# A one-core decoder trunk: buffer rings of five panels, sums first in seven-product squares, low-rank stages moved

## The chip, the cores and the metric

The kernel runs on one core of a Trainium2 chip. The metric is the device time of one execution in microseconds; before the change it is 1195.39 us, the median of three runs (1192.28 to 1196.88). In the profile PE is TensorE's matmul, PEld its weight loads, DVE VectorE, ACT ScalarE, POOL GpSimd and SP the engine that issues most DMAs.

## The reference

One layer on 256 tokens of width 2048, in float32. The input projection feeds a pooling mixer and an RWKV-7 mixer of 16 heads of 64; a squared-ReLU FFN of width 8192 and a gated embedding follow.

```python
h = rms_norm(x, attn_norm)
z = h @ w_in
zs = token_shift(z[..., POOL_WIDTH:IN_WIDTH], mu_shift)      # r, k, v, then the low-rank w, a, g
d = causal_multiscale_pool(z[..., :POOL_WIDTH])
pool_out = einsum('btgc,gcd->btgd', d, pool_w) * pool_scale
# rwkv7_time_mix:
decay = exp(-exp(-softplus(-(w0 + tanh(zw) @ w_up)) - 0.5))
a = sigmoid(a0 + za @ a_up);  g = sigmoid(zg) @ g_up
kk = normalized(k * k_k);  k = k * (1 + (a - 1) * k_a)
y = wkv7_scan(r, decay, k, v, -kk, kk * a)                   # a recurrence over the tokens
y = group_norm(y) * gn_g + gn_b + sum(r * k * r_k) * v
x = x + concat([pool_out, y * g]) @ w_out
x = x + square(relu(rms_norm(x, mlp_norm) @ w_ffn_up)) @ w_ffn_down
x = x + sigmoid(rms_norm(x, ple_norm) @ w_ple_gate) * (p @ w_ple_proj)
return rms_norm(x, final_norm)
```

## The kernel before

Weights come from HBM as panels of 128 x 1024 floats (512 KB). `load_raw` issues the load on SP's queue into a "raw" buffer. `split_w` splits the panel in a high part (`wh`, a copy on ACT in two halves, L165) and a low part (`wl`, raw less high, on DVE, L166). The activations are split in the same way, and each product is three matmuls: high by high, low by high, high by low. The buffers come from rings: `ring` takes one of three `wp` buffers of its tag, and once the pool `fp` exists (in the FFN and after it) every fourth request takes a buffer from that pool, so a ring has four there.

**The front part** overlaps two kinds of work on PE. Products of z are generators in a list `queue`: zk0, zr0, zk1, zr1, zv0, zv1, then the pool products zp0, zp1 (k, r and v for the two groups of eight heads, 0 and 1). `fill(us)` lets the head of the list emit matmuls worth that many us by its own estimate, `finish(p)` empties the list up to the end of one product. Between them stand the calls of the RWKV stages, written by hand. `rwkv_lora(gi)` makes the decay's running products `P` and `EI` and the rate `aa` of one group: two pairs of matmul groups `lw` and `la` (L521), eight sigmoids on ACT (L524, L525), four scans on DVE (L528) and two Exp (L530, L531). `rwkv_k` squares k (L542), sums per head on PE (`kkn`), takes the norm, spreads it (`rnb`), and builds the factors `AR` and `BK` of the scores (L560 to L584). `rwkv_scores` (L613) and `rwkv_scores_half` (L642) multiply them, `rwkv_sources` makes transposed sources, `bonus_sums` (`bsum`) and `bonus` (`bon`, L755) the bonus term, `rwkv_values` (`vt`, L769) the centred values. `rwkv_core` runs the recurrence in chunks of 64 tokens; `group_norm` (L880 to L884) scales its output and `group_out` (`yt`, L890) transposes it. When a product of z ends, its two PSUM banks are emptied by L322 on ACT and L323 on DVE.

**The FFN** goes by halves of the hidden width. `gemm_wide` makes the up product. `sweep` makes the down product, two times for each half (d00, d01, d10, d11), over 16 pairs of panels each. Pairs 1, 3, ..., 13 are squares by seven products in place of eight: `weights_seven` forms four sums `t` of blocks of the two raw panels `ra` and `rb` (L1226, L1231, L1232), high parts (`ha`, `hb` in the wh ring, `th`) and low parts (`la`, `lb` in the wl ring, L1229 and L1235; `tl`, L1236). The other pairs are plain (`split_w`). The residual of a sweep is formed in a tile `u`.

**The tail** makes the gate's product with eight panels kept in SBUF (`keep`), in buffers that the FFN has left, and the final norm.

What orders the instructions of an engine: the framework's scheduler places them by the order of the program and by priority. `tc.high_priority(n)` moves instructions ahead on their engine. A buffer is reused when its last reader is done, and the wait for that stands in the engine's queue, in order.

Of the kernel before, what the change touches and what calls it, by code (L numbers as in the profile page):

```python
# [9 lines left out]
F32 = mybir.dt.float32  # L10
F32R = mybir.dt.float32r
AF = mybir.ActivationFunctionType
ALU = mybir.AluOpType
# [27 lines left out]
def trunk(  # L41
# [19 lines left out]
    nc = tc.nc  # L61
# [81 lines left out]

    extra = []
    turns = {"raw": 0, "wh": 0, "wl": 0, "mm": 0}

    def ring(tag, dt, name):

        if extra:
            turns[tag] += 1  # L150
            if turns[tag] % 4 == 0:
                return extra[0].tile([128, 1024], dt, tag=f"{tag}x", name=name)
        return wp.tile([128, 1024], dt, tag=tag, name=name)

    def load_raw(src, n, name):
        raw = ring("raw", F32, f"raw_{name}")
# [852 lines left out]

    fill(3.0)  # L1010
    wag_out()
    fill(14.0)
    st0 = rwkv_lora(0)
    finish(p_zk0)
    wband = make_bands()
    rwkv_k(0, st0, zk0[0])
    finish(p_zr0)
    rwkv_r(0, st0, zr0[0])
    fill(7.0)
    rwkv_scores(0, st0)  # L1020
    rwkv_sources(0, st0)
    bonus_sums(0, st0)
    st1 = rwkv_lora(1)
    finish(p_zk1)
    rwkv_k(1, st1, zk1[0])
    fill(12.0)
    rwkv_scores_half(1, st1, 0)
    sts = (st0, st1)
    beside += [inverse(sts), 1.0, 0.0]
# [3 lines left out]
    rwkv_scores_half(1, st1, 1)  # L1033
    rwkv_sources(1, st1)
    finish(p_zv0)
    fill(4.0)
    rwkv_values(0, st0, zv0[0])
    bonus_sums(1, st1)
    while beside:
        fill(1.0)  # L1040
    fill(2.4)
# [9 lines left out]
    ds0 = pool_chunk(0, zt0[0])  # L1051
    for gi in range(2):
        group_out(gi, 0, norms[0][gi], YTs[gi])
    fill(4.0)
    for gi in range(2):
        group_out(gi, 1, norms[1][gi], YTs[gi])
    mgs = []
# [92 lines left out]
        nc.vector.reciprocal(s2, s2)  # L1150

    kept = []
    keep_at = ["ys"] * 3 + ["a5", "th", "tl", "t", "U"]

    def keep():
        kp = len(kept)
        where = keep_at[kp]
        raw = load_raw(w_gate[3, kp].rearrange("p a n -> p (a n)"), 1024, f"gk{kp}")
        if where == "ys":
            wh, wl = (fp.tile([128, 1024], F32R, tag=where, bufs=7, name=f"gk{kp}{c}") for c in "hl")  # L1160
# [55 lines left out]
    def weights_seven(ra, rb, name):  # L1216

        b12, b21, b22 = rb[:, 0:512], rb[:, 512:1024], ra[:, 512:1024]
        t, th, tl = (
            fp.tile([128, 4, 512], dt, tag=tg, name=f"{tg}_{name}") for tg, dt in (("t", F32), ("th", F32R), ("tl", F32R))  # L1220
        )
        ha, hb = (ring("wh", F32R, f"w7h{i}_{name}") for i in range(2))
        la, lb = (ring("wl", F32R, f"w7l{i}_{name}") for i in range(2))
        with tc.high_priority(20000):
            nc.scalar.activation(ha, ra, AF.Copy)
            nc.vector.tensor_tensor(  # L1226
                t[:, 0:2], ra.rearrange("p (c n) -> p c n", c=2), b12.unsqueeze(1).to_broadcast([128, 2, 512]), op=ALU.subtract
            )
            nc.vector.tensor_tensor(la, ra, ha.bitcast(F32), op=ALU.subtract)  # L1229
            nc.scalar.activation(th[:, 0:2], t[:, 0:2], AF.Copy)  # L1230
            nc.vector.tensor_tensor(t[:, 2], b22, t[:, 0], op=ALU.add)  # L1231
            nc.vector.tensor_tensor(t[:, 3], b21, t[:, 2], op=ALU.subtract)  # L1232
            nc.scalar.activation(hb[:, 0:512], b21, AF.Copy)
            nc.scalar.activation(th[:, 2:4], t[:, 2:4], AF.Copy)  # L1234
            nc.vector.tensor_tensor(lb[:, 0:512], b21, hb[:, 0:512].bitcast(F32), op=ALU.subtract)  # L1235
            nc.vector.tensor_tensor(tl, t, th.bitcast(F32), op=ALU.subtract)  # L1236

        def half(h_, l_, c):
            return h_[:, c * 512 : (c + 1) * 512], l_[:, c * 512 : (c + 1) * 512]

        return {
            "b11": half(ha, la, 0), "b22": half(ha, la, 1), "b21": half(hb, lb, 0),
            **{nm: (th[:, c], tl[:, c]) for c, nm in enumerate(("t1", "t3", "t2", "t4"))},
        }

    def sweep(src, acts, np_, name, residual_, hooks=()):
# [22 lines left out]
        for i in range(npair):  # L1269
# [3 lines left out]
            if i in SEVEN:  # L1273
# [8 lines left out]
                    ):  # L1282
                        step(which, o, a(f), w[t], fin and which != "p4")
                if fin:
                    u = fp.tile([128, 4, 512], F32, tag="U", name=f"u_{name}")
                    with tc.high_priority(30000):
                        nc.scalar.activation(u[:, 0], p1, AF.Copy)
                        nc.vector.tensor_tensor(u[:, 1], p6, u[:, 0], op=ALU.add)
# [16 lines left out]

    def scaled_residual(n, tt, src, wide=512):
        xs = xr[tt][:, n * 512 : n * 512 + wide]
        with tc.high_priority(10000 if wide > 512 else 30000):
            nc.vector.scalar_tensor_tensor(xs, src, s2[:, tt : tt + 1], xs, op0=ALU.mult, op1=ALU.add)

    def ffn_half(hf):
# [187 lines left out]
```

## Time and profile before

| | us |
| --- | --- |
| runs | 1195.39, 1196.88, 1192.28 (median 1195.39) |
| the profiled execution | 1192.48 |
| its span | 1190.8 |
| PE, PEld busy | 1164.7, 996.4 |
| DVE, ACT busy | 855.4, 678.7 |
| granted TensorE clock, mean | 0.997 |

The span runs from the first to the last instruction; the rest of the 1192.48 lies around it. Busy time is the union of an engine's instructions; matmuls overlap in PE, and their ends are modelled, so their cadence is read from starts. A row of the waits names the engine and line that waited, what it waited for, the sum in us, how often, and the longest. A row of the timeline has the start, the duration in us, the engine, the line, the operation, its output and inputs, and in brackets the idle time in front of it with what ended it.

The windows of the trace give PE's busy time by stage, from the span's start:

```text
window            PE busy   DVE busy  ACT busy
0 to 130          120.17    92.64     90.83      start, zk0, zr0, zk1, part of zr1
130 to 325        190.65   134.41    116.25      rest of the mixers, first part of w_out
325 to 570        244.84   157.32    129.43      w_out, first FFN up
570 to 1090       516.55   410.96    285.23      FFN: down 0, up 1, down 1
1090 to 1191       92.53    60.07     56.94      gate, final norm
```

### The profile page before, as it was taken

The page shows a single profiled execution, that of the slowest core. Times are in us where ns is not written, and L with a number is a line of the kernel's source. Part 1 is how long each engine was busy: PE and PEld are TensorE (multiplying, and loading weights), DVE is VectorE, ACT ScalarE, POOL GpSimd, SP SyncE. Part 2 cuts the span into 40 slices and gives each one's busy share as a digit, 9 for nine tenths or more (in the row PEclk, how much of TensorE's full clock was granted, in tenths as well). Part 3 has the DMA queues.
Part 4 walks back from the last instruction along what each step waited for, and adds up shares of the span by engine and source line. Part 5 has one row for each costly group of instructions (what it writes and reads, how often), then busy time and mean ns, then how long its engine had stood idle before and what let it go on. Part 6 is the DMA issues. An engine that isn't in the chain of part 4 may idle for free.

```text
span 1190.8 us, 18955 instructions
## 1 busy us (share of the span) xinstructions
PE 1164.7 (98%) x7366; PEld 996.4 (84%) x7366; DVE 855.4 (72%) x1073; ACT 678.7 (57%) x1210; POOL 20.1 (2%) x77
## 2 busy tenths in 40 slices
PE   7999999999999999999999999999999999999997
PEld 5899999787888888888878888888888788887886
DVE  6885799356655666667788887666668789888753
ACT  5956765667555554555554554554546554568643
POOL 4100000000000000000000000000000000000000
PEclk9999999999999999999999999999999999999999
DMA  7353434454566556565455656555555565666831
GB/s 267 124 187 124 155 125 142 143 175 138 191 184 191 178 180 191 182 190 182 172 212 185 217 204 210 193 181 190 185 187 163 208 208 186 218 246 201 274 125 71
DMA packets 60618, 216.92 MB, mean 182 GB/s; under 512 B 6768, under 2 KB 7536, under 8 KB 60144
## 3 DMA queue, kind: packets, MB, share of 16 engines
q1 hardware_dynamic: 60240, 215.20, 54.8%
q8 instruction: 58, 0.95, 0.3%
q10 hardware_dynamic: 288, 0.51, 0.1%
q14 instruction: 32, 0.26, 0.1%
HBM read 213.59 MB, written 2.10 MB: 181 GB/s over the span
## 4 chain that ended last, share of the span: by engine, by line
PE 73%; DVE 5%; DMA 2%; ACT 1%; issue 1%; DVEq 0%; ACTq 0%
PE u_w L1104 20%; PE d_p L1173 13%; PE u_w L1108 10%; PE d_w L1173 5%; PE d_d L1173 3%; PE o_b L188 2%; PE o_b L187 2%; PE o_b L189 2%; PE gt_b L187 2%; PE gt_b L189 2%; PE gt_b L188 2%; DVE wl_d L166 2%; DMA raw_d<-in_w_ffn_down_dram 2%; PE zp_b L187 1%; PE zp_b L189 1%
## 5 line engine op out<-in xcount | busy, mean ns | idle before, releaser
L1104 PE MATMUL u_w<-h,wh_u 128*128 128x512 f32 x1024 | 362.1, 399 | 0.0
L1108 PE MATMUL u_w<-h,wl_u 128*128 128x256 f32 x1024 | 287.7, 281 | 0.0
L165 ACT ACTIVATE wh_u<-raw_u 128x512 fp32r<-128x512 f32 x256 | 147.4, 624 | 175.6 <-issue 136.7
L166 DVE TENSOR_TENSOR wl_u<-raw_u,wh_u 128x1024 fp32r<-128x1024 f32 x128 | 156.6, 1224 | 120.9 <-ACT wh_u L165 120.9
L1104 PEld LDWEIGHTS u_w<-h,wh_u 128*128 128x128 f32 x1024 | 192.5, 188 | 47.8
L1108 PEld LDWEIGHTS u_w<-h,wl_u 128*128 128x128 f32 x1024 | 193.4, 189 | 0.0
L1173 PE MATMUL d_p<-wh_d,yd 128*128 128x512 f32 x432 | 115.6, 389 | 0.0
L1173 PEld LDWEIGHTS d_p<-wh_d,yd 128*128 128x128 f32 x432 | 81.0, 188 | 16.6
L165 ACT ACTIVATE wh_d<-raw_d 128x512 fp32r<-128x512 f32 x144 | 79.7, 619 | 23.4 <-PE d_d L1173 12.0
L166 DVE TENSOR_TENSOR wl_d<-raw_d,wh_d 128x1024 fp32r<-128x1024 f32 x72 | 85.1, 1219 | 2.3 <-ACT wh_d L165 2.2
L1236 DVE TENSOR_TENSOR tl_d<-t_d,th_d 128x2048 fp32r<-128x2048 f32 x28 | 64.2, 2292 | 29.3 <-ACT th_d L1234 29.3
L1173 PE MATMUL d_p<-wl_d,yd 128*128 128x512 f32 x216 | 68.5, 393 | 2.8 <-DVE wl_d L166 2.8
L1234 ACT ACTIVATE th_d<-t_d 128x1024 fp32r<-128x1024 f32 x28 | 29.7, 1060 | 69.1 <-DVE t_d L1232 69.1
L166 DVE TENSOR_TENSOR wl_o<-raw_o,wh_o 128x1024 fp32r<-128x1024 f32 x32 | 39.1, 1225 | 35.9 <-ACT wh_o L165 35.9
L165 ACT ACTIVATE wh_o<-raw_o 128x512 fp32r<-128x512 f32 x64 | 36.7, 624 | 32.4 <-PE o_b L188 18.4
L1173 PEld LDWEIGHTS d_p<-wl_d,yd 128*128 128x128 f32 x216 | 40.5, 188 | 14.2 <-DVE wl_d L166 6.1
L1226 DVE TENSOR_TENSOR t_d<-raw_d,raw_d 128x1024 f32<-128x1024 f32 x28 | 34.2, 1222 | 14.4 <-DMA raw_d<-in_w_ffn_down_dram 14.4
L1173 PE MATMUL d_w<-th_d,ys 128*128 128x512 f32 x168 | 42.6, 389 | 0.0
L1230 ACT ACTIVATE th_d<-t_d 128x1024 fp32r<-128x1024 f32 x28 | 29.7, 1060 | 17.9 <-DVE t_d L1226 14.7
L178 PE MATMUL zv_b<-hTh,wh_zv 128*128 128x256 f32 x128 | 37.8, 295 | 1.3 <-DVE zv_t L323 1.3
L178 PE MATMUL zr_b<-hTh,wh_zr 128*128 128x256 f32 x128 | 36.7, 287 | 2.0 <-DVE zk_t L323 2.0
L1173 PE MATMUL d_d<-wh_d,yd 128*128 128x512 f32 x144 | 38.5, 389 | 0.0
(445 smaller groups left out, 2529.5 us busy)
## 6 DMA issues: line engine op xcount, KB each, us to landing
raw_u<-in_w_ffn_up_dram SPq DMA_DIRECT2D x128, 512.0 KB, 3.5
raw_d<-in_w_ffn_down_dram SPq DMA_DIRECT2D x128, 512.0 KB, 4.4
raw_o<-in_w_out_dram SPq DMA_DIRECT2D x32, 512.0 KB, 3.5
raw_gt<-in_w_ple_gate_dram SPq DMA_DIRECT2D x24, 512.0 KB, 4.4
raw_zk<-in_w_in_dram SPq DMA_DIRECT2D x16, 512.0 KB, 4.1
raw_zr<-in_w_in_dram SPq DMA_DIRECT2D x16, 512.0 KB, 3.5
raw_zv<-in_w_in_dram SPq DMA_DIRECT2D x16, 512.0 KB, 3.5
raw_zp<-in_w_in_dram SPq DMA_DIRECT2D x16, 512.0 KB, 3.5
```

The costliest lines, as they stand in the source:

```text
L165: nc.scalar.activation(wh[:, a * 512 : (a + 1) * 512], raw[:, a * 512 : (a + 1) * 512], AF.Copy)
L166: nc.vector.tensor_tensor(wl, raw, wh.bitcast(F32), op=ALU.subtract)
L178: nc.tensor.matmul(o, w_h, ah, start=first and ct % 2 == 0, stop=False, skip_group_check=True)
L187: nc.tensor.matmul(o, a_h, wh[:, 0:n], start=first, stop=False)
L188: nc.tensor.matmul(o, a_l, wh[:, 0:n], start=False, stop=False)
L189: nc.tensor.matmul(o, a_h, wl[:, 0:n], start=False, stop=last)
L1104: nc.tensor.matmul(bank[:, ct, :].rearrange("p (s t) -> p s t", s=2), wh[:, c], hl, start=k == 0, stop=False, skip_group_check=True,)
L1108: nc.tensor.matmul(bank[:, ct, 0:T], wl[:, c], hl[:, 0, :], start=False, stop=k == 15, skip_group_check=True)
L1173: nc.tensor.matmul(o, l, r, start=first, stop=last, skip_group_check=True)
L1226: nc.vector.tensor_tensor(t[:, 0:2], ra.rearrange("p (c n) -> p c n", c=2), b12.unsqueeze(1).to_broadcast([128, 2, 512]), op=ALU.subtract)
L1230: nc.scalar.activation(th[:, 0:2], t[:, 0:2], AF.Copy)
L1236: nc.vector.tensor_tensor(tl, t, th.bitcast(F32), op=ALU.subtract)
```

## The change

Six edits, in the order of the program. (a) The rings of raw and wh get two buffers from `fp` in place of one (five in all); wl keeps three and one. Within a ring the extra buffers are now named by their turn, and turns are counted from the start. (b) The stages of group 0 and 1: `rwkv_lora(0)` moves behind `finish(p_zk0)` and `make_bands`, with two new fills of 3; the fill of 14 ahead of it goes. `rwkv_lora(1)` moves ahead of `rwkv_sources(0)`, and the fill ahead of the first half of the scores of group 1 goes from 12 to 13. (c) `bonus_sums(1)` moves ahead of `rwkv_values(0)`. (d) The fill between the two pairs of `group_out` goes from 4 to 5.3. (e) In `weights_seven` the two sums come before the low parts in the program. (f) `u` takes the buffer of `t`; the tag "U" goes, one kept gate panel has its low part in "yd", and the wide residual's priority is 25000.

```diff
     extra = []
     turns = {"raw": 0, "wh": 0, "wl": 0, "mm": 0}
+    RING = {"raw": (3, 2), "wh": (3, 2), "wl": (3, 1)}
 
     def ring(tag, dt, name):
 
-        if extra:
-            turns[tag] += 1
-            if turns[tag] % 4 == 0:
-                return extra[0].tile([128, 1024], dt, tag=f"{tag}x", name=name)
-        return wp.tile([128, 1024], dt, tag=tag, name=name)
+        n, m = RING[tag]
+        turns[tag] += 1
+        if extra and turns[tag] % (n + m) >= n:
+            return extra[0].tile([128, 1024], dt, tag=f"{tag}x", bufs=m, name=name)
+        return wp.tile([128, 1024], dt, tag=tag, bufs=n, name=name)
...
     wag_out()
-    fill(14.0)
-    st0 = rwkv_lora(0)
     finish(p_zk0)
     wband = make_bands()
+    fill(3.0)
+    st0 = rwkv_lora(0)
+    fill(3.0)
     rwkv_k(0, st0, zk0[0])
     finish(p_zr0)
     rwkv_r(0, st0, zr0[0])
     fill(7.0)
     rwkv_scores(0, st0)
+    st1 = rwkv_lora(1)
     rwkv_sources(0, st0)
     bonus_sums(0, st0)
-    st1 = rwkv_lora(1)
     finish(p_zk1)
     rwkv_k(1, st1, zk1[0])
-    fill(12.0)
+    fill(13.0)
     rwkv_scores_half(1, st1, 0)
...
     finish(p_zv0)
+    bonus_sums(1, st1)
     fill(4.0)
     rwkv_values(0, st0, zv0[0])
-    bonus_sums(1, st1)
...
         group_out(gi, 0, norms[0][gi], YTs[gi])
-    fill(4.0)
+    fill(5.3)
     for gi in range(2):
         group_out(gi, 1, norms[1][gi], YTs[gi])
...
-    keep_at = ["ys"] * 3 + ["a5", "th", "tl", "t", "U"]
+    keep_at = ["ys"] * 3 + ["yd", "a5", "th", "tl", "t"]
...
-            nc.vector.tensor_tensor(la, ra, ha.bitcast(F32), op=ALU.subtract)
-            nc.scalar.activation(th[:, 0:2], t[:, 0:2], AF.Copy)
             nc.vector.tensor_tensor(t[:, 2], b22, t[:, 0], op=ALU.add)
             nc.vector.tensor_tensor(t[:, 3], b21, t[:, 2], op=ALU.subtract)
+            nc.scalar.activation(th[:, 0:2], t[:, 0:2], AF.Copy)
             nc.scalar.activation(hb[:, 0:512], b21, AF.Copy)
+            nc.vector.tensor_tensor(la, ra, ha.bitcast(F32), op=ALU.subtract)
+            nc.vector.tensor_tensor(lb[:, 0:512], b21, hb[:, 0:512].bitcast(F32), op=ALU.subtract)
             nc.scalar.activation(th[:, 2:4], t[:, 2:4], AF.Copy)
-            nc.vector.tensor_tensor(lb[:, 0:512], b21, hb[:, 0:512].bitcast(F32), op=ALU.subtract)
             nc.vector.tensor_tensor(tl, t, th.bitcast(F32), op=ALU.subtract)
...
-                    u = fp.tile([128, 4, 512], F32, tag="U", name=f"u_{name}")
+                    u = fp.tile([128, 4, 512], F32, tag="t", name=f"u_{name}")
...
-        with tc.high_priority(10000 if wide > 512 else 30000):
+        with tc.high_priority(25000 if wide > 512 else 30000):
```

How this moves instructions is shown at three places. A row has the line, the operation, the output and the inputs, the shape, and a count where equal rows follow each other; numbers behind a name tell buffers apart. Lines of the changed kernel are one to three higher than before. First ACT, in the seam from zk0 to zr0, before: `lw` and `la` are the low-rank products, L322 empties the banks of zk0.

```order
L165 ACTIVATE wh_zr_0_690<-raw_zr_0_688 128x512 x2
L524 ACTIVATE tA_t<-lw,par_sb 128x256 x2
L525 ACTIVATE tD_t<-la,par_sb 128x256 x2
L564 ACTIVATE tE_t<-tD_t,oka,par_sb 128x256 x2
L524 ACTIVATE tA_t<-lw,par_sb 128x256 x2
L525 ACTIVATE tD_t<-la,par_sb 128x256 x2
L530 ACT_TABLE_LOAD
L530 ACTIVATE tA_t<-tB_t 128x1024
L165 ACTIVATE wh_zr_1_721<-raw_zr_1_719 128x512 x2
L322 ACTIVATE zk_t<-zk_b_339,omu 128x256
L531 ACTIVATE tC_t<-tB_t 128x1024
L322 ACTIVATE zk_t<-zk_b_340,omu 128x256
```

The same stretch of ACT in the changed kernel (L323 here is L322 of before):

```order
L166 ACTIVATE wh_zr_0_648<-raw_zr_0_646 128x512 x2
L166 ACTIVATE wh_zr_1_679<-raw_zr_1_677 128x512 x2
L323 ACTIVATE zk_t<-zk_b_339,omu 128x256 x2
L323 ACTIVATE zk_t<-zk_b_340,omu 128x256
L166 ACTIVATE wh_zr_2_744<-raw_zr_2_742 128x512 x2
L323 ACTIVATE zk_t<-zk_b_340,omu 128x256
L166 ACTIVATE wh_zr_3_783<-raw_zr_3_781 128x512 x2
L525 ACTIVATE tA_t<-lw,par_sb 128x256 x2
L526 ACTIVATE tD_t<-la,par_sb 128x256 x2
```

The copies out of zk0's banks now stand ahead of the low-rank stage. Second PE, around the transposes `yt` of the second half of the tokens, before:

```order
L890 MATMUL yt<-ident,ys_2747 128x128 x4
L187 MATMUL zp_b_2928<-wh_zp_7_3330,hTh_153 128x512
L188 MATMUL zp_b_2928<-wh_zp_7_3330,hTl_155 128x512
L189 MATMUL zp_b_2928<-wl_zp_7_3331,hTh_153 128x512
L187 MATMUL zp_b_2928<-wh_zp_7_3330,hTh_153 128x512
L188 MATMUL zp_b_2928<-wh_zp_7_3330,hTl_155 128x512
L189 MATMUL zp_b_2928<-wl_zp_7_3331,hTh_153 128x512
L890 MATMUL yt<-ident,ys_2746 128x128 x4
```

and in the changed kernel (L891 is L890 of before):

```order
L952 MATMUL pd_3399<-wband,zt_2899 128x128
L891 MATMUL yt<-ident,ys_2752 128x128 x4
L891 MATMUL yt<-ident,ys_2753 128x128 x4
L891 MATMUL yt<-ident,ys_2752 128x128 x4
L891 MATMUL yt<-ident,ys_2753 128x128 x4
L910 MATMUL gt<-zf,gu_2721 128x256 x4
```

The six matmuls of zp1 no longer stand between the two pairs of transposes; they come earlier. Third DVE, in the first down sweep, one square (pair 5) and the plain pair 4 ahead of it, before:

```order
L1226 TENSOR_TENSOR t_d_5_6166<-raw_d_0_5_6162,raw_d_1_5_6164 128x1024
L166 TENSOR_TENSOR wl_d_0_4_6129<-raw_d_0_4_6124,wh_d_0_4_6128 128x1024
L166 TENSOR_TENSOR wl_d_1_4_6134<-raw_d_1_4_6126,wh_d_1_4_6133 128x1024
L1229 TENSOR_TENSOR w7l_d_5_6171<-raw_d_0_5_6162,w7h_d_5_6169 128x1024
L1231 TENSOR_TENSOR t_d_5_6166<-raw_d_0_5_6162,t_d_5_6166 128x512
L1235 TENSOR_TENSOR w7l_d_5_6172<-raw_d_1_5_6164,w7h_d_5_6170 128x512
L1232 TENSOR_TENSOR t_d_5_6166<-raw_d_1_5_6164,t_d_5_6166 128x512
L1236 TENSOR_TENSOR tl_d_5_6168<-t_d_5_6166,th_d_5_6167 128x2048
```

and in the changed kernel (L1229, L1232, L1233 are the sums, L1236 and L1237 the low parts, L1239 is L1236 of before):

```order
L1229 TENSOR_TENSOR t_d_5_6166<-raw_d_0_5_6162,raw_d_1_5_6164 128x1024
L1232 TENSOR_TENSOR t_d_5_6166<-raw_d_0_5_6162,t_d_5_6166 128x512
L167 TENSOR_TENSOR wl_d_0_4_6129<-raw_d_0_4_6124,wh_d_0_4_6128 128x1024
L167 TENSOR_TENSOR wl_d_1_4_6134<-raw_d_1_4_6126,wh_d_1_4_6133 128x1024
L1233 TENSOR_TENSOR t_d_5_6166<-raw_d_1_5_6164,t_d_5_6166 128x512
L1236 TENSOR_TENSOR w7l_d_5_6171<-raw_d_0_5_6162,w7h_d_5_6169 128x1024
L1237 TENSOR_TENSOR w7l_d_5_6172<-raw_d_1_5_6164,w7h_d_5_6170 128x512
L1239 TENSOR_TENSOR tl_d_5_6168<-t_d_5_6166,th_d_5_6167 128x2048
```

The sums moved ahead of the low parts, which now lie between the last sum and `tl`. Eight squares, pairs 3 to 9 of d01 and d11, keep the order of before on DVE.

More of the change, by code (lines that the diff above doesn't have):

```diff
@@ L1158, in keep @@
         raw = load_raw(w_gate[3, kp].rearrange("p a n -> p (a n)"), 1024, f"gk{kp}")
-        if where == "ys":
-            wh, wl = (fp.tile([128, 1024], F32R, tag=where, bufs=7, name=f"gk{kp}{c}") for c in "hl")
+        if where[0] == "y":
+            wh = fp.tile([128, 1024], F32R, tag="ys", bufs=7, name=f"gk{kp}h")
+            wl = fp.tile([128, 1024], F32R, tag=where, bufs=7 if where == "ys" else 1, name=f"gk{kp}l")
         else:
```

## The prediction

> **What bounds the kernel now.** I read the page's busy times first, then the chain that ended last, then the waits of TensorE.
>
> ```profile
> PE 1164.7 (98%) x7366; PEld 996.4 (84%) x7366; DVE 855.4 (72%) x1073; ACT 678.7 (57%) x1210; POOL 20.1 (2%) x77
> PE 73%; DVE 5%; DMA 2%; ACT 1%; issue 1%; DVEq 0%; ACTq 0%
> ```
>
> ```profile
> PE wag_b L359 <- DMA wag<-in_w_wag_dram: 7.8, 1, 7.8
> PE d_p L1173 <- DVE wl_d L166: 2.8, 6, 0.6
> PE zr_b L178 <- DVE zk_t L323: 2.0, 1, 2.0
> PE sc L642 <- DVE AR L584: 1.4, 1, 1.4
> PE zv_b L178 <- DVE zv_t L323: 1.3, 1, 1.3
> PE yt L890 <- DVE gv L883: 1.2, 1, 1.2
> PE h3t L1125 <- DVE h L1132: 0.6, 1, 0.6
> PE yt L890 <- DVE ys L884: 0.2, 1, 0.2
> ```
>
> PE is busy for 98% of the span and carries most of the chain. The change leaves its matmuls as they are: the same number, shapes and operands, in another order. So it can only touch the time in which PE waits. The columns of the waits are the sum in us, how often, and the longest. The first one, 7.8 us, is the start, before any line that is edited. What is left, 2.8 + 2.0 + 1.4 + 1.3 + 1.2 + 0.6 + 0.2, is 9.5 us or 0.8% of the span: **that is all there is to win**, and every term below is one of these waits taken away, moved or made anew.
>
> **1. The low-rank stage of group 0, behind k.** At the seam from zk0 to zr0:
>
> ```profile
> 49.99 1.28 ACT L530 ACT_TABLE_LOAD   x1
> 52.33 1.14 ACT L165 ACTIVATE wh_zr<-raw_zr 128x512 fp32r<-128x512 f32 x2
> 53.37 0.46 ACT L322 ACTIVATE zk_t<-zk_b,omu 128x256 f32<-128x256 f32 x1
> 54.64 1.01 DVE L323 SCALAR_TENSOR_TENSOR zk_t<-zk_b,par_sb,zk_t 128x255 f32<-128x255 f32 x2
> ...
> 56.59 0.39 PE L178 MATMUL zr_b<-hTh,wh_zr 128*128 128x256 f32 x1 [1.99 <-DVE zk_t L323]
> ```
>
> The second half of zr0 writes a bank that L322 on ACT and L323 on DVE still have to empty. The first of these copies starts on ACT at 53.37, behind the sigmoids, a table load and the Exp (L530) of the low-rank stage (ACT is one queue). In the new order nothing but the copies of zr0's panels stands before them, and the sigmoids come after. I take off the whole **2.0**; bounds 0.9 (one panel copy of 1.14 that PE still has to wait out) and 2.0. What may be late next is group 0 itself: the kkn sums and the rnb spread of `rwkv_k` move two to three panels back in the z stream, and the first scores do not. Adding the durations that the same DVE instructions have in before, set behind the later rnb without a gap, their chain ends 1.5 us ahead of those scores: an estimate, and a rival below.
>
> **2. The low-rank stage of group 1, ahead of group 0's sources.** Here the wait is on the last pieces of AR:
>
> ```profile
> DVE tB_t L560 <- ACT tC_t L531: 1.1, 1, 1.1
> ```
>
> ```profile
> 124.11 1.28 ACT L531 ACT_TABLE_LOAD   x1
> 125.40 1.06 ACT L531 ACTIVATE tC_t<-tB_t 128x1024 f32<-128x1024 f32 x1
> ...
> 137.33 1.22 DVE L166 TENSOR_TENSOR wl_zv<-raw_zv,wh_zv 128x1024 fp32r<-128x1024 f32 x1
> 138.86 0.18 DVE L584 TENSOR_SCALAR AR<-tB_t 128x16 f32<-128x16 f32 x1
> 139.19 1.07 PE L642 MATMUL sc<-AR,BK 64*128 64x64 f32 x15 [1.39 <-DVE AR L584]
> ```
>
> The Exp of L531 ends at 126.46 because a square root (L551) came between it and the first Exp, and each change of function cost a table load of 1.28. DVE waits 1.1 for it at L560, and L584 is the tail of that queue. With the stage moved, both Exp's come together, two of the loads are gone (2.6 us of ACT), and L584 now stands ahead of two subtractions for zv0 (1.22 each) that it followed. Together that is 1.1 + 2.4 = 3.5 us against a wait of 1.39; and `fill(13)` puts nine more matmuls of 0.12 (1.1 us) ahead of the scores. I take off **1.4**; bounds 0.7 and 1.4.
>
> **3. bonus_sums(1) ahead of rwkv_values(0).**
>
> ```profile
> 175.99 0.39 PE L178 MATMUL zv_b<-hTh,wh_zv 128*128 128x256 f32 x1 [1.34 <-DVE zv_t L323]
> 179.05 0.71 PE L489 MATMUL bon<-bs,hsel 32*128 32x256 f32 x8
> 179.69 2.05 PE L769 MATMUL vt<-cen,zv_t 128*128 128x128 f32 x16
> 181.68 0.64 PE L478 MATMUL bsum<-tF_t,jsel 128*32 128x256 f32 x8
> 179.98 1.41 DVE L755 TENSOR_TENSOR ybuf<-bon,zv_t 128x256 f32<-128x256 f32 x4
> ```
>
> The bsum matmuls, 0.64 us, move from 181.68 into the wait of 1.34 before 175.99, whose releaser is not changed: -0.64. But bsum now takes one of the small PSUM banks first, so that the bank that vt wants is the one of the first bon. DVE empties it at L755, which started at 179.98; one of its four takes 0.35. So vt would start near 180.35, not 179.69: +0.66. I take **0**; bounds -0.7 and +0.7. The instruction behind the waiting vt on PE is the zv1 stream, and nobody else waits for it.
>
> **4. `fill(5.3)` between the two yt pairs.**
>
> ```profile
> 272.64 1.04 PE L890 MATMUL yt<-ident,ys 128*128 128x128 f32 x8
> 273.74 0.39 PE L188 MATMUL zp_b<-wh_zp,hTl 128*128 128x512 f32 x1
> 273.97 0.40 PE L189 MATMUL zp_b<-wl_zp,hTh 128*128 128x512 f32 x1
> ...
> 276.28 0.63 PE L890 MATMUL yt<-ident,ys 128*128 128x128 f32 x4 [1.22 <-DVE gv L883]
> 275.44 0.69 DVE L884 TENSOR_TENSOR ys<-ys,gv 128x512 f32<-128x512 f32 x1
> ```
>
> This one goes the other way. The second pair of yt waits for a chain of small steps on ACT and DVE that PE's dy started. In before, the last six zp1 matmuls, 0.23 apart (273.74 to 273.97), covered 1.4 us of that chain. The new order has none there: the number in the call is larger, but the queue it draws from is empty, as earlier fills took more. The six matmuls are not saved; they run where PE did not wait. So the wait grows from 1.4 to about 2.8: **+1.4**; bounds +0.5 (the zt copy and a panel copy, 0.6 each on ACT, now lie earlier) and +1.5.
>
> **5. The down sweeps: five panels, sums first.** PE's six waits there, 2.8 us, are for a plain panel's low part.
>
> ```profile
> L1236 DVE TENSOR_TENSOR tl_d<-t_d,th_d 128x2048 fp32r<-128x2048 f32 x28 | 64.2, 2292 | 29.3 <-ACT th_d L1234 29.3
> DVE t_d L1226 <- DMA raw_d<-in_w_ffn_down_dram: 14.4, 13, 1.8
> ```
>
> ```profile
> 593.19 1.23 DVE L1226 TENSOR_TENSOR t_d<-raw_d,raw_d 128x1024 f32<-128x1024 f32 x1 [1.72 <-DMA raw_d<-in_w_ffn_down_dram]
> 594.33 2.35 DVE L166 TENSOR_TENSOR wl_d<-raw_d,wh_d 128x1024 fp32r<-128x1024 f32 x2
> 596.60 1.22 DVE L1229 TENSOR_TENSOR w7l_d<-raw_d,w7h_d 128x1024 fp32r<-128x1024 f32 x1
> ...
> 598.94 0.68 DVE L1232 TENSOR_TENSOR t_d<-raw_d,t_d 128x512 f32<-128x512 f32 x1
> ```
>
> One plain pair and one square are 24 + 21 matmuls, 45 x 0.23 = 10.4 us of PE. DVE needs for them 1.23 + 2.35 + 1.22 + 3 x 0.68 (L1232, and L1231 and L1235 of the same shape) + 2.29 = 9.1, less 0.08 that neighbours overlap (594.33 + 2 x 1.22 is 596.77, and the second ends at 596.68), five times: 8.7. To this before adds 1.1 for th (the 29.3 in the row of L1236, over 26 waits) and, in 13 squares, 1.1 for raw (14.4 over 13): 10.9, more than PE's 10.4, and what is late then is the wl behind L1226. In the new order L1229 and L1235's work stands between L1232 and L1236, 1.8 us, which hides the 1.1 in the squares that take it: 20 of the 28. In eight of the second and fourth sweep the scheduler kept the old order. With the 1.1 gone, DVE has 8.7 + 1.1 = 9.8 at worst, under PE's 10.4. I take off **2.3** (20/28 of 2.8 is 2.0; a fifth raw panel and the boundary between sweeps give a little more); bounds -2.8 and +14 (the last rival).
>
> ```profile
> 641.13 1.22 DVE L1290 TENSOR_TENSOR u_d<-u_d,d_w 128x1024 f32<-128x1024 f32 x1
> 642.38 2.48 DVE L1309 SCALAR_TENSOR_TENSOR x<-u_d,s2sq,x 128x1024 f32<-128x1024 f32 x2
> ```
>
> The new order also puts sums that read each other side by side. Neighbours that don't depend on each other start 0.08 before the other ends (594.33, two in 2.35); L1309, which reads L1290's output, starts 0.03 after its end. So each such pair costs DVE 0.11, up to 0.22 a square, inside its slack. The Trainium skill (VectorE: DVE Perf Modes, "The DRAIN you can't avoid") says that the pipeline empties after every operation and that a semaphore between two costs nothing extra; by it the order would be free and the sum unchanged, while these rows show a difference, so I go by them.
>
> **6. The rest.** The kept gate panels and u change buffers: no instruction is added, and the 0.6 of h3t stays. Its bounds are -0.6 and +1.
>
> **The sum**: -2.0 - 1.4 + 0 + 1.4 - 2.3 = -4.3 us. The profiled execution took 1192.48 (its span of 1190.8 and 1.7 around it), so 1188.2; it lies 2.9 under the median of the three runs, 1195.39, and beside that median the changed kernel is **1191.1**.
>
> **The rivals.**
> - *All waits go* (-2.0 - 1.4 - 0.7 + 0.5 - 2.8 = -6.4, with h3t -7.0): near 1188.5. For it: ACT and DVE have 28% and more to spare. Against it: yt.
> - *The sweeps stay as they are*: -2.0, so 1193.4. The wait of L1226 for raw stays, as a wl that lies behind three sums is later than one behind L1226 alone. Rows for it: L1226's waits of up to 1.8.
> - *Group 0's scores come too early* for the moved chain. The margin is 1.5 us; beyond it each us of DVE is one of PE. I give it 2 us: 1193.
> - *Slower: the raw ring of five.* The second panel of a square now gets the buffer that held the first one of the square before, and its last reader, L1229, now comes late: up to 1.23 + 0.68 + 2.35 + 0.68 + 1.22 = 6.2 after the square's start instead of 4.7 (593.19 to the end of L1229, 597.82). The row below gives 4.4 for a landing: 10.6 in all, against PE's 10.4. Above that point each square is late by the difference, and L1226 holds the wl's behind it. With landings of 4.9, 0.7 in each of 20 squares is 14; with the sweep's gain lost and the rest kept, -2.0 + 14 = +12: 1207.
>
> ```profile
> raw_d<-in_w_ffn_down_dram SPq DMA_DIRECT2D x128, 512.0 KB, 4.4
> ```
>
> **How the numbers follow.** About 6 us, 0.5%, is what a measurement of this kernel can tell from no change. Chances: my forecast 0.37, all waits go 0.26, sweeps unchanged 0.20, scores late 0.08, the ring 0.09. Faster by more than 0.5% is under 1189.4: most of the second case and the lower edge of the first, 0.33. Slower is over 1201.4, the ring alone: 0.08. The rest is 0.59. The range goes from 1186.0 (all waits, and the runs' own scatter of about 2.5) to 1198.0 (unchanged sweeps, the upper bounds of terms 3 and 4 and that scatter); it leaves out the ring.
>
> **What would show it.** In the changed kernel's waits of PE: zr_b and sc gone; zv_b near 0.7 and a new vt near 0.7 on L755; yt near 2.8; d_p under 1. DVE's wait for th should fall from 29.3 to about 9. If d_p grows, or DVE's wait for raw_d is far over 14.4, the ring is the reason; a new sc on the first scores would mean the moved chain. If PE's waits sum to much less or more than 13 us while the time does not follow, the view itself was wrong.

## The result and the profile after

The changed kernel takes 1188.99 us, the median of six runs (1187.15 to 1189.55); before, six runs beside it, 1195.53. The ratio is 0.9953, with a 95% interval of 0.9938 to 0.9968: 0.47% faster. That ratio is the record's own and not the quotient of the two medians, which is 0.9945 (6.5 us). The forecast was 1191.1 in a range of 1186 to 1198, so the number held. Most of its terms did not hold in the way they were argued, as the trace shows. Times here and below are medians of fast runs: of the twelve runs of raw_ring_only one took 6577.01 us and is left out as a slow one.

The waits of PE in the changed kernel, in the columns of before (waited for; us in total, times, longest):

```profile
PE wag_b L360 <- DMA wag<-in_w_wag_dram: 7.7, 1, 7.7
PE yt L891 <- DVE gv L884: 3.1, 1, 3.1
PE zk_b L179 <- DVE zr_t L324: 2.2, 1, 2.2
PE zp_b L188 <- DVE zv_t L324: 1.6, 1, 1.6
PE vt L770 <- DVE ybuf L756: 0.9, 1, 0.9
PE rnb L490 <- DVE rnq L554: 0.8, 2, 0.7
PE d_p L1176 <- DVE wl_d L167: 0.6, 1, 0.6
PE us L846 <- ACT UV L839: 0.4, 1, 0.4
PE zv_b L179 <- DVE zv_t L324: 0.4, 1, 0.4
PE yt L891 <- DVE ys L885: 0.2, 1, 0.2
```

zr_b and sc are gone, d_p fell from 2.8 to 0.6, yt grew to 3.3, and vt and zv_b together are what zv_b was. But zk_b, zp_b and rnb are new. The rows sum to 17.9; those of before that the prediction shows to 17.3, and 17.7 with two more of 0.2. **The waits of PE did not shrink at all, and yet the profiled execution is 3.1 us shorter** (1189.38 against 1192.48). By the forecast's own last sign (waits far from 13 us that the time does not follow) the view of the waits alone does not give the time.

The rnb wait is two waits, the short one in the stage of group 0 and the long one in that of group 1:

```profile
73.42 0.71 PE L490 MATMUL rnb<-rnq,hsel 32*128 32x256 f32 x8 [0.18 <-DVE rnq L554]
126.57 0.71 PE L490 MATMUL rnb<-rnq,hsel 32*128 32x256 f32 x8 [0.67 <-DVE rnq L554]
```

DVE's wait for th fell from 29.3 to 15.1, where the forecast said 9, and its wait for raw grew from 14.4 to 18.2:

```profile
DVE t_d L1229 <- DMA raw_d<-in_w_ffn_down_dram: 18.2, 12, 3.2
DVE tl_d L1239 <- ACT th_d L1238: 15.1, 17, 1.4
```

The page has the rest in the busy time:

```profile
PE 1161.4 (98%) x7366; PEld 996.2 (84%) x7366; DVE 857.2 (72%) x1073; ACT 675.0 (57%) x1208; POOL 20.1 (2%) x77
```

PE is busy 3.3 us less (1164.7 before) for the same 7366 matmuls. The start of the first matmul of each product, from the timeline of the two kernels, gives the time of each stage (us):

```text
stage                                    before    after   difference
start to zk0's first matmul                26.5     27.4     +0.9   (ahead of every edit)
zk0 to w_out's first matmul               259.9    263.0     +3.1
w_out                                      95.7     95.9     +0.2
FFN up, first half                        181.7    178.4     -3.3
FFN down, first half                      167.8    166.2     -1.6
FFN up, second half                       180.9    180.9      0.0
FFN down, second half                     166.3    164.4     -1.9
tail, to the last matmul                  103.4    103.0     -0.4
```

So in these two executions the front part lost 3 us where 2 had been forecast to be won, the sweeps won 3.5 where 2.3 had been forecast, and 3.3 came from the first up product, for which there was no term. No edit touches its matmuls; its panels do pass through the rings that became deeper.

**A wait has a second price.** The windows of the changed kernel around the gates, behind the yt wait (columns: us, then the busy time of PE, PEld, DVE, ACT and POOL with instructions, the granted TensorE clock, the DMA share and GB/s):

```profile
278.60:279.80 1.20, 0.99 (x8) 0.78 (x9) 0.67 (x1) 1.20 (x5) 0.00 (x0) 1.00 0.03 10
279.80:280.30 0.50, 0.50 (x5) 0.41 (x4) 0.00 (x0) 0.50 (x3) 0.00 (x0) 0.69 0.00 0
280.30:283.00 2.70, 2.70 (x8) 1.92 (x6) 2.41 (x4) 2.34 (x7) 0.00 (x0) 0.50 0.00 0
283.00:283.50 0.50, 0.50 (x3) 0.19 (x4) 0.36 (x1) 0.00 (x0) 0.00 (x0) 0.59 0.00 0
283.50:284.50 1.00, 1.00 (x9) 0.61 (x9) 0.00 (x0) 0.00 (x0) 0.00 (x0) 1.00 0.00 0
```

and the rows of PE there in the timeline:

```profile
278.57 0.63 PE L891 MATMUL yt<-ident,ys 128*128 128x128 f32 x4 [3.07 <-DVE gv L884]
279.88 3.51 PE L910 MATMUL gt<-zf,gu 128*128 128x256 f32 x8
284.40 1.99 PE L910 MATMUL gt<-zf,gu 128*128 128x256 f32 x8
```

After a wait of 3.07 us the granted clock falls to 0.50 for 3.4 us, and the first eight gate matmuls take 3.51 us, where the other eight take 1.99. So the lost cover at yt cost 1.9 us of wait and 1.6 of half clock. The same is in before, behind the wait of 1.39 us at sc:

```profile
139.20:141.00 1.80, 1.80 (x32) 1.80 (x32) 1.77 (x4) 1.61 (x4) 0.00 (x0) 1.00 0.92 289
141.00:142.00 1.00, 1.00 (x9) 0.93 (x8) 1.00 (x3) 0.00 (x0) 0.00 (x0) 0.77 0.58 217
142.00:144.00 2.00, 2.00 (x12) 2.00 (x11) 2.00 (x3) 0.00 (x0) 0.00 (x0) 0.50 0.69 178
144.00:145.00 1.00, 1.00 (x7) 1.00 (x7) 0.32 (x1) 0.00 (x0) 0.00 (x0) 0.52 0.53 213
```

A stretch of 3.4 us at half the clock does the work of 1.7 us: by this estimate it adds 1.7 us (at the gates 1.6 were measured), and the view of waits has no row for it, since PE is busy. The page's line of the clock, with 40 slices of 30 us, shows 9 throughout.

**A second cadence in the up product.** The rows of PE in the first up product, before:

```profile
450.10 0.40 PE L1104 MATMUL u_w<-h,wh_u 128*128 128x512 f32 x1
450.34 0.28 PE L1108 MATMUL u_w<-h,wl_u 128*128 128x256 f32 x1
450.46 0.40 PE L1104 MATMUL u_w<-h,wh_u 128*128 128x512 f32 x1
450.69 0.28 PE L1108 MATMUL u_w<-h,wl_u 128*128 128x256 f32 x1
450.81 0.40 PE L1104 MATMUL u_w<-h,wh_u 128*128 128x512 f32 x1
```

and after:

```profile
449.89 0.39 PE L1106 MATMUL u_w<-h,wh_u 128*128 128x512 f32 x1
450.12 0.28 PE L1110 MATMUL u_w<-h,wl_u 128*128 128x256 f32 x1
450.24 0.39 PE L1106 MATMUL u_w<-h,wh_u 128*128 128x512 f32 x1
450.47 0.28 PE L1110 MATMUL u_w<-h,wl_u 128*128 128x256 f32 x1
450.59 0.39 PE L1106 MATMUL u_w<-h,wh_u 128*128 128x512 f32 x1
```

Two pairs take 0.71 us before (450.10 to 450.81) and 0.70 after (449.89 to 450.59). Behind the first eighth of the half, which is slower in both, a pair takes 353.3 ns before and 346.7 after; over 512 pairs that would be 3.4 us, the whole difference. There is no wait in either. In the second up product both kernels run at 353.3.

### The profile page after: what moved, and what is told of

Same layout as the page of the kernel before. It is cut to its first block, busy times and chain, and to the rows that moved or that the text cites. A ratio compares the mean times of both kernels' runs of the same rounds, so it can differ in the third digit from the quotient of the medians.

```text
span 1187.6 us, 18920 instructions
## 1 busy us (share of the span) xinstructions
PE 1161.4 (98%) x7366; PEld 996.2 (84%) x7366; DVE 857.2 (72%) x1073; ACT 675.0 (57%) x1208; POOL 20.1 (2%) x77
## 4 chain that ended last, share of the span: by engine, by line
PE 91%; DVE 4%; ACT 2%; DMA 1%; issue 1%; ACTq 0%; DVEq 0%
PE u_w L1106 20%; PE d_p L1176 17%; PE u_w L1110 10%; PE d_w L1176 6%; PE d_d L1176 4%; PE o_b L189 2%; PE o_b L188 2%; PE o_b L190 2%; PE gt_b L188 2%; PE gt_b L190 2%; PE gt_b L189 2%; PE wag_b L360 2%; PE zp_b L188 1%; PE zk_b L179 1%; PE zk_b L180 1%; PE zk_b L181 1%
## 5 line engine op out<-in xcount | busy, mean ns | idle before, releaser
L166 ACT ACTIVATE wh_d<-raw_d 128x512 fp32r<-128x512 f32 x144 | 82.1, 622 | 65.5 <-PE d_d L1176 39.7
L1239 DVE TENSOR_TENSOR tl_d<-t_d,th_d 128x2048 fp32r<-128x2048 f32 x28 | 64.1, 2290 | 15.1 <-ACT th_d L1238 15.1
L1229 DVE TENSOR_TENSOR t_d<-raw_d,raw_d 128x1024 f32<-128x1024 f32 x28 | 34.2, 1222 | 18.3 <-DMA raw_d<-in_w_ffn_down_dram 18.2
L1228 ACT ACTIVATE w7h_d<-raw_d 128x1024 fp32r<-128x1024 f32 x28 | 29.5, 1053 | 24.2 <-PE d_d L1176 22.8
L167 DVE TENSOR_TENSOR wl_zp<-raw_zp,wh_zp 128x1024 fp32r<-128x1024 f32 x16 | 19.6, 1223 | 27.6 <-ACT wh_zp L166 24.8
L179 PE MATMUL zk_b<-hTh,wh_zk 128*128 128x256 f32 x128 | 37.3, 291 | 2.2 <-DVE zr_t L324 2.2
```

The lines of the kernel that those rows point to most:

```text
L179: nc.tensor.matmul(o, w_h, ah, start=first and ct % 2 == 0, stop=False, skip_group_check=True)
L1229: nc.vector.tensor_tensor(t[:, 0:2], ra.rearrange("p (c n) -> p c n", c=2), b12.unsqueeze(1).to_broadcast([128, 2, 512]), op=ALU.subtract)
```

## The experiments

In the table the time is the median of the runs, the one of before is from runs on the same chip beside them, and the stages are from each kernel's profile as above: "front" is zk0 to w_out, "up 0" the first up product, "down" the two down halves together.

```text
kernel               time     before   ratio (95%)               front   up 0    down
before               1195.53           1                         259.9   181.7   334.1
the change           1188.99  1195.53  0.9953 (0.9938-0.9968)    263.0   178.4   330.6
front_only           1195.96  1194.03  1.0012 (0.9995-1.0028)    263.4   181.7   333.2
ffn_only             1186.83  1194.03  0.9944 (0.9922-0.9966)    259.8   181.8   330.5
ffn_lora1            1186.63  1194.03  0.9942 (0.9922-0.9961)    261.8   181.7   329.6
yt_cover             1186.68  1194.03  0.9927 (0.9906-0.9948)    263.5   178.4   329.6
rings_only           1190.02  1194.34  0.9960 (0.9944-0.9976)    261.4   178.4   329.5
sums_only            1196.14  1194.34  1.0009 (0.9991-1.0027)    263.3   181.7   335.6
merge_cover          1185.49  1194.34  0.9917 (0.9888-0.9947)    258.1   181.7   330.0
lora0_early          1183.44  1194.34  0.9904 (0.9875-0.9932)    256.6   181.7   330.1
lora0_back           1183.04  1194.50  0.9896 (0.9876-0.9917)    258.0   181.8   329.0
early_old_squares    1184.06  1194.50  0.9900 (0.9877-0.9923)    256.8   181.8   330.6
raw_ring_only        1194.16  1194.50  0.9995 (0.9980-1.0011)    261.4   181.7   333.4
early_bonus_back     1181.82  1194.50  0.9879 (0.9860-0.9899)    257.0   181.8   329.4
```

A stage is from one execution of each kernel, so the scatter of a stage matters. Five kernels have the front part of before (before, ffn_only, rings_only, sums_only, raw_ring_only) and take 259.8 to 263.3 us in it. Most of that is half-clock stretches: with 1.7 us taken off for each one, four of them take 258.0 to 258.2. sums_only takes 259.9, with longer waits at yt and dy and no edit near them. The change and front_only, treated alike, take 261.3 and 261.7.

**front_only** is the kernel of before with the calls of the front part as changed, and nothing else.

> The edits of the front part alone (low-rank stages, bonus sums, fills), with the rings, the squares and the tail of before. The reading of the two traces by stage: the front part of the changed kernel reaches the FFN 4.1 us later than before's (of which 0.9 lies ahead of every edit), and the gains of 3.3 in the first up product and 3.5 in the two down halves come behind it. By this reading this kernel is 3 to 4 us slower than before, with yt waiting near 3.1 and the gates' matmuls at half the clock. The rival, the prediction on record: zr and sc gone, yt up by 1.4, so 2.0 us faster than before. Second rival on the first up product: if its 3.3 us come from a place that the front part shifts, they show here too, and the two cancel: same time as before.

Its front takes 263.4 us, 3.5 more than before's, with yt waiting 3.8 and zk_b 2.2, and the clock at about half in the windows from 278 to 282. The profiled execution is 2.8 us slower than that of before (1195.31 against 1192.48), the medians differ by 1.9, and the interval of the ratio reaches just below 1. The forecast's direction (faster) is out; the size of the loss is between nothing and 3 us by the timed runs, and about 3 us by the fronts without their half-clock stretches.

**ffn_only** is the changed kernel with the calls of the front part as before.

> The edits of the rings, squares, kept panels and residual alone, with the front part of before. By stages: the down halves take 3.5 us less than before (each 166.2 and 164.6 against 167.8 and 166.5), and if the fast first up product (178.4 against 181.7 us) comes from the rings it shows again, 6.8 us faster than before in all; if it is a state that can fall either way, 3.5 us faster, or 6.8 with the fast state. The prediction on record had 2.3 for the down sweeps.

The down halves take 166.1 and 164.4, 3.6 less in all. The first up product ran at the slow cadence in its profile, so it is not the FFN's edits that make it fast each time. The median is 7.2 us below before, more than the stages of one execution show (4.4 between the two profiled executions); its ten runs go from 1182.0 to 1192.8.

**ffn_lora1** adds to ffn_only the move of `rwkv_lora(1)`, the fill of 13, and this:

```diff
-    fill(3.0)
+    fill(1.6)
     norms = rwkv_core(sts)
```

> As the kernel with the FFN's edits alone, with the low-rank stage of group 1 moved ahead of group 0's sources and the fill of 13 behind it, and the fill ahead of the core cut from 3.0 to 1.6 so that six matmuls of zp1 still stand between the yt pairs. If the wait of sc L642 (1.4 us) was the table loads and the two subtractions ahead of AR, it is gone and this kernel is 1.4 us faster than the one with the FFN's edits alone. Rival: the work that covered it is missing later (a new wait in zv, zp or gm): no faster.

The rival held. sc's wait is gone, but zp_b waits 1.9 and rnb of group 1 0.7 in its place, and the time is that of ffn_only (1186.63 and 1186.83). Its front has two half-clock stretches, behind zr_b and zp_b, where that of ffn_only has one. Work that a fill draws early is missing where it covered something later.

**yt_cover** is the changed kernel with the same edit of that fill.

> The changed kernel with the fill ahead of the core at 1.6 in place of 3.0: six matmuls of zp1 stand between the yt pairs again. Theory: in the changed kernel the missing cover cost 1.9 us of wait at yt and 1.6 more, because after a wait of 3.1 us the granted clock fell to 0.5 for 3.4 us and the gates' matmuls took 3.5 us in place of 1.9. Then this kernel is 3 to 3.5 us faster than the changed one, with yt near 1.4 and the clock at 1.0 in the gates. Rival: the work is missing at the place that it was taken from (the start of the core), and the time is the same; or only the wait returns to 1.4 and the clock falls all the same: 1.4 to 1.9 faster.

yt waits 1.2 + 0.2 again, and no half-clock stretch lies at the gates. The median is 7.35 us below before's, where the changed kernel was 6.5 below its own: less than the 3 to 3.5 expected, with intervals that overlap. The front of the profiled execution is no shorter (263.5), because two other half-clock stretches fell in it, 3.4 us behind zk_b at 82 to 87 and 6.8 us behind zp_b at 204 to 213: 5.1 us by the estimate above, without which it would be 258.4. A stretch is a matter of the single execution: the same wait has one in one profile and none in another.

**rings_only** is ffn_only with the squares in the old order, and **sums_only** is before with the squares in the new order.

> Before, with the rings of five for raw and wh, u in the buffer of t, the kept panels and the residual's priority, and the squares in the old order. With both FFN edits the two down halves took 166.1 and 164.4 against 167.8 and 166.3 (3.6 us less). If the deeper raw ring did it, this kernel has DVE's wait for raw at L1226 down from 14.4 and most of the 3.6; if the sums-first order did it, the wait for th stays at 29 and the halves stay within 0.6 of before. The last rival of the prediction, the second panel waiting for the first one's buffer, would make the wait for raw grow here too, but less than with sums first, as L1229 comes early.

> Before, with the sums ahead of the low parts and nothing else. The prediction's step: the wait for th falls from 29 to 15 or less, and with it DVE's time for a plain pair and a square falls under PE's, so that this alone gives 2.0 to 2.8 us in the two down halves. Rival: without the fifth raw buffer the second panel of a square is freed at the same place, and the wait for raw takes what th gives: under 0.8.

The rings alone take 4.6 us off the down halves, and all of the d_p waits. The sums first alone take nothing off; the halves are 1.5 longer in all, and DVE's waits are these:

```profile
DVE t_d L1226 <- DMA raw_d<-in_w_ffn_down_dram: 21.3, 16, 3.7
DVE tl_d L1236 <- ACT th_d L1235: 20.9, 26, 1.1
```

What th gives back (29.3 to 20.9), raw takes (14.4 to 21.3), as the rival of the expectation said. rings_only has the same wait for th (21.1), 16.2 for raw, and no row for d_p in PE's waits. So the wait for th was not what decided. In time rings_only is 3.2 us above ffn_only, with intervals that overlap; its halves are no longer (329.5 against 330.5), so this is not the order of the sums showing in the sweeps. Over all 14 profiles the two halves take 329.0 to 330.6 us in the ten kernels with both rings at five, in either order of the sums, and 333.2 to 335.6 in the other four.

A late wl costs more than its row says. Two neighbouring matmuls of before's first down half:

```profile
595.60 0.50 PE L1173 MATMUL d_p<-wl_d,yd 128*128 128x512 f32 x1
596.74 0.50 PE L1173 MATMUL d_p<-wl_d,yd 128*128 128x512 f32 x1 [0.64 <-DVE wl_d L166]
```

They start 1.14 us apart where 0.23 is usual: 0.91 us lost for a row of 0.64. Six such rows make the 2.8 of d_p; the two halves of before are 5.1 us longer than those of lora0_back, which has no such row.

**raw_ring_only** asks which ring it was:

```diff
-    RING = {"raw": (3, 2), "wh": (3, 2), "wl": (3, 1)}
+    RING = {"raw": (3, 2), "wh": (3, 1), "wl": (3, 1)}
```

> As the kernel with the rings alone, with the wh ring at three and one again: only raw has five. If the raw ring is the cause (a panel loaded earlier), the halves stay near 165.1 and 164.4; if the wh ring is (the copies on ACT wait for PE to free a buffer), they go back towards 167.8 and 166.3, with PE's waits for wl_d at 2 to 3 us again.

With raw at five and wh at four the gain is gone: 0.9995, and 333.4 for the halves against 334.1 (one shorter by 2.1, one longer by 1.4). The profiles of this kernel and of rings_only also differ in the first up product (181.7 and 178.4), so the halves are the cleaner comparison. The groups of the high copies, first of this kernel and then of rings_only (the last columns are the idle time of ACT ahead of them, and what ended it):

```profile
L166 ACT ACTIVATE wh_d<-raw_d 128x512 fp32r<-128x512 f32 x144 | 79.0, 620 | 59.5 <-PE d_d L1175 52.9 <-issue 5.8 <-DMA raw_d<-in_w_ffn_down_dram 0.7
```

```profile
L166 ACT ACTIVATE wh_d<-raw_d 128x512 fp32r<-128x512 f32 x144 | 82.4, 622 | 55.5 <-PE d_d L1175 31.9 <-DMA raw_d<-in_w_ffn_down_dram 13.2 <-issue 9.6
```

With raw at five and wh at four the copy waits 52.9 us in all for PE to let go of a wh buffer; with both at five 31.9, and 13.2 for loads. In before, with four of each, it waited 12.0. PE's d_p waits are 2.3 in the first and none in the second. So beside a raw ring of five it takes the fifth wh buffer; whether that does it without the fifth raw one was not tried. The sum of the copy's waits does not order the three kernels, so it is not the cause by itself. What stands ahead of a late wl is a wait for raw, here in raw_ring_only:

```profile
970.88 2.19 ACT L166 ACTIVATE wh_d<-raw_d 128x512 fp32r<-128x512 f32 x4 [4.72 <-PE d_d L1175]
973.12 1.23 DVE L1228 TENSOR_TENSOR t_d<-raw_d,raw_d 128x1024 f32<-128x1024 f32 x1 [2.13 <-DMA raw_d<-in_w_ffn_down_dram]
975.71 2.35 DVE L167 TENSOR_TENSOR wl_d<-raw_d,wh_d 128x1024 fp32r<-128x1024 f32 x2
978.12 0.50 PE L1175 MATMUL d_p<-wl_d,yd 128*128 128x512 f32 x1 [0.52 <-DVE wl_d L167]
```

All five late wl's of this kernel have such a wait for raw (1.39 to 2.65 us) 4 to 5 us ahead of them, and ahead of it, in four of the five, a copy that waited 3.4 us or more for PE. In before five of the six have it (1.25 to 1.72 us) too. The likely chain is copy late, raw buffer freed late, next load late; it is read from the rows and no edit shows it.

**merge_cover** moves the cut of yt_cover to the merge:

```diff
-    fill(2.4)
+    fill(1.0)
     rwkv_merge(sts)
```

> The changed kernel with the fill ahead of the merge at 1.0 in place of 2.4, so that twelve matmuls of zv1 stand between the first two pieces of the merge, and nine of zp1 between the yt pairs. Theory: in the changed kernel the fills ran out of zv1 before the merge, and zp0's first matmuls waited 1.6 us for zv1's banks to be emptied; here that wait is gone as well as the cover of yt restored: yt under 0.8, zp_b under 0.5, no half clock in the gates, 4.5 to 5 us under the changed kernel in the front part. Rival: the wait at zp_b was a free one, and the merge itself (its copies on ACT) takes its place: 3.5 only.

The wait at zp_b falls to 0.2 and that at yt to 0.6 + 0.2; two of 0.4 and 0.3 come up at dy. Its front takes 258.1, 4.9 less than the changed kernel's, as expected, without a half-clock stretch (1.7 of the 4.9). The merge did not take the place of the wait.

**lora0_early** also takes out the fill of 3 between `rwkv_lora(0)` and `rwkv_k(0)`.

> As the kernel with the cover ahead of the merge, without the fill of 3 between the low-rank stage of group 0 and rwkv_k, so that kkn and rnb come one panel earlier in zr0. Theory: the 2.2 us that zk1 waited for zr0's banks (L324 of the changed kernel) are DVE's four products behind rnb, two of 1.2 and a panel's subtraction that stood in its queue at the end of zr0; a panel earlier (3.2 us of PE) they are done by then, and the wait falls from 2.2 to under 0.5. Rival: rnb then waits for its own chain on ACT and DVE (0.7 already), up to 3 us more, and the sum is no smaller.

The front is another 1.5 shorter, but not for the reason given: zk_b still waits 2.0. The timeline of DVE there:

```profile
75.95 1.22 DVE L167 TENSOR_TENSOR wl_zk<-raw_zk,wh_zk 128x1024 fp32r<-128x1024 f32 x1
77.09 1.22 DVE L580 TENSOR_TENSOR BK<-tF_t,tC_t 128x1024 f32<-128x1024 f32 x1
78.23 1.22 DVE L167 TENSOR_TENSOR wl_zk<-raw_zk,wh_zk 128x1024 fp32r<-128x1024 f32 x1
79.36 0.47 DVE L324 SCALAR_TENSOR_TENSOR zr_t<-zr_b,par_sb,zr_t 128x255 f32<-128x255 f32 x1
```

The scores' factors are spread over the whole seam, one between each two panels, and L324 stands in a queue without a gap wherever rnb comes. What fell is rnb (0.9 to 0.7), dy (0.7 to none) and 0.2 of zk_b; that is 1.1 of the 1.5.

**lora0_back** is merge_cover with `rwkv_lora(0)` and its fill of 14 at the place of before.

> The kernel with the cover ahead of the merge, with the low-rank stage of group 0 at its place of before (its fill of 14 too). It tells what that move alone was worth. The prediction on record: 2.0 us, so this kernel would be 2.0 slower than the one with the cover. The reading of the traces: the move takes the 2.0 us wait off zr0 and makes one of 2.2 at zk1 and 0.9 at rnb, so this kernel is within 1 us of it, or up to 1 us faster; whether a half-clock stretch (1.7 us) follows the wait in a run weighs on both alike.

1183.04 against 1185.49 with the move, with intervals that overlap; the fronts are equal (258.0 and 258.1), though this one has a half-clock stretch at 58 to 61 and the other has none; without that stretch its front would be the shorter one by about 1.8. The forecast's 2.0 for this move is out: it carried the wait from one seam to the next. rnb still waits 0.7 here, so that wait does not come from this move, as the expectation had it.

**early_old_squares** is lora0_early with the squares of before, **early_bonus_back** is lora0_early with `bonus_sums(1)` behind `rwkv_values(0)` as before.

> The kernel with the cover and rwkv_k early, with the squares of before (low parts between the sums). Rings alone took 4.6 us off the down halves and sums first alone nothing (2.0 more than before's), so by the rings theory this kernel has the same two halves (164.6 and 165.5, each within 0.6) and the same time as with sums first. The prediction on record has sums first as the larger part: then the halves are 2 us longer here.

> The kernel with the cover and rwkv_k early, with bonus_sums(1) behind rwkv_values(0) as in before. The prediction on record has this move at zero: the wait at vt (0.9) goes, the one at zv comes back to 1.3 from 0.3, and the time is within 0.5 us. Rival: with bonus_sums(1) late the bonus of group 1 and its bs on ACT come later, and the second vt waits: up to 1 us slower.

The first has the halves at 166.2 and 164.4, one 1.7 longer and one 1.1 shorter than lora0_early's, 0.6 us more in all, and a median 0.6 us above lora0_early's, in another set of runs: with both rings at five the order of the sums decides nothing that these runs can tell. The second has vt without a wait and zv_b at 1.1, and its front is 0.4 longer; its median is the lowest of all, 1181.82, 0.9879 of before. That is below the changed kernel's interval: a version that beats both.

## Why the prediction was right

The number was right because errors of both signs nearly met, and that is luck: two terms left out the waits that came in place of those that they took away, one was too small by more than half, one named the wrong cause, and 3.3 us came from no term. By its own steps:

1. *Low-rank stage of group 0, -2.0.* zr_b's wait went as foreseen. What came next was looked for in the wrong place: I priced the first scores, which never waited, and left out the other seam. rwkv_k's products now stand in DVE's queue when zr0's banks must be emptied: zk_b 2.2, and 0.2 at rnb of group 0. In waits the step was worth +0.4, and lora0_back shows it as no gain.
2. *Low-rank stage of group 1, -1.4.* sc's wait went, and with it the half-clock stretch behind it, 1.7 more in this execution. But the fill of 13 and the stage's move took zv1 matmuls from the merge: zp_b, 1.6; and rnb of group 1 now waits 0.7. Both waits are in ffn_lora1, which shows a net of nothing; that fills draw from one list, which step 4 had seen, was not carried over to here.
3. *bonus_sums(1), 0.* vt 0.9 and zv_b 0.4 stand against 1.3 and 0.2. Right, in both of its parts; early_bonus_back agrees.
4. *The yt pairs, +1.4.* The wait grew by 1.9, and the half clock behind it added 1.6. The mechanism was right, and half of its price was missing.
5. *Down sweeps, -2.3.* They gave 3.5, and the step that failed is the cause: "sums first" hides the wait for th, and DVE's total falls under PE's. sums_only gives nothing, and rings_only all of it. The forecast took th for the cause, where the row that stands ahead of the late wl's is L1226's wait for raw. It laid out the raw ring and never asked what the wh ring on the same path does: raw_ring_only, with raw alone at five, gains nothing. Its size was off too, as it priced d_p by its rows of 2.8, where the halves had 5.1 to give. That the fifth raw buffer makes squares wait (the slower rival) was right in its direction, 14.4 to 18.2 at L1229, but PE is late behind one of those waits only: d_p 0.6. Why the others no longer reach PE with both rings at five stays open.
6. *The rest.* h3t's 0.6 is gone, inside the bound.
7. *The sum.* "All there is to win" counted rows of waits, and left out the clock behind a wait, the time that a late matmul loses beyond its row, and the up product. By its own terms the upper end of the range is 1196.7, not 1198.0, as the 1193.4 of the unchanged sweeps already has 1.4 for yt in it; the result lies far from it. The 4.7 in the rival on the raw ring is 4.6 (593.19 to 597.82); nothing hangs on it.

The fast first up product (-3.3) was in no term. Added up for the two profiled executions: +3.1 and +0.9 ahead of it, +0.2, -3.3, -3.5, -0.4 is -3.0, against -3.1. The timed runs differ by more, 6.5 us. Half-clock stretches are a part of it: the five profiles with before's front all have one behind the sc wait, and three of them another behind zr_b. Of the 17 runs of before beside the last set, the five with a mean granted clock of 0.997 took 1190.7 to 1194.5 us, and the five at 0.993 or 0.994 took 1194.1 to 1199.1; the profiled one of before has 0.997. So before probably loses 1.7 us at each of two waits in some runs (a timed run does not show where), and its profiled execution was one of the quicker ones. The change took both places away and made others (zk_b, zp_b, yt). How much of the 6.5 these and the second cadence make can't be read from timed runs, and stays open.

## What to carry to other kernels

Where an engine is busy for 98%, list its waits, and price each one twice: by its row, and by what the clock does behind it, which only windows of a few us show. Work used as cover is a budget: a fill added in one place is missing in another, so follow the list to its end before taking a wait off the sum. When a ring is deepened, look for every ring on the same path (here raw and wh), as the shallowest one may take over the wait, and raw at five with wh at four gained nothing here.

## What was not expected of the hardware

- The granted clock fell to 0.50 after PE waits of 1.39 us (before, sc), about 2 us (zr_b, in rings_only from 58 to 61) and 3.07 us (the change, yt); each stretch lasted about 3.4 us and began within 2.5 us of the wait's end; in yt_cover one behind zp_b (1.6 us) lasted 6.8. The length of the wait does not decide it: in the 14 profiles the sc wait of 1.4 has one 5 times in 5, the zr_b wait of 2.0 5 times in 7, and the zk_b wait of 2.0 to 2.2 once in 7. The Trainium skill (TensorE: Matmul & The Clock Gate, "HAM oscillation — how this bites in real kernels") gives as the abstract rule that PE have no idle gaps over about 3.4 us; here the clock fell behind shorter ones, two of them with small matmuls right behind (the transposes of yt, the 64x64 scores).
- The pair of a 128x512 and a 128x256 matmul in the up product ran at 353.3 or at 346.7 ns on average, for a whole half, without a wait in either. In the 14 profiles the first half was fast three times (the change, yt_cover, rings_only) and the second never. All three have both rings at five, but so do seven with the slow one; no run here settles what chooses.
